# Conditioning columns as a 128-column moving operand, token loads ahead of modulation tiles, and planner costs taken from measured durations

## The chip, the cores and the metric

The kernel runs on one core of a Trainium2 chip. The metric is the device time of one execution in microseconds (us). The kernel before takes 1305.76 us, the median of three runs (1305.68 to 1306.54). Engines are called as in the profile: PE is TensorE's matmul stream, PEld its weight loads, DVE VectorE, ACT ScalarE, POOL GpSimd, SP SyncE (which issues most of the DMAs).

## The reference, cut to what matters

One layer on 512 latent tokens and 256 context tokens, width 1024, all in float32. Every sub-layer reads an RMS-normed stream that is scaled and shifted by a modulation, which is a matrix product of SiLU of a conditioning vector with one 1024 x 9216 matrix. There are two conditioning vectors: one for the tokens, one for the context.

```
mod_lat = (silu(c)     @ w_mod + b_mod)          # 9 vectors of 1024
mod_ctx = (silu(c_ctx) @ w_mod + b_mod)
adaln(h, i) = rms_norm(h) * g * (1 + mod[3i+1]) + mod[3i]
x   = x   + 0.5 * mod_lat[2] * swiglu(adaln(x, 0))      # first FFN, 2816 hidden
ctx = ctx + 0.5 * mod_ctx[2] * swiglu(adaln(ctx, 0))
y   = mixer(adaln(x, 1), adaln(ctx, 1))                 # S5 scan heads + 4 differential attention heads
x   = x + mod_lat[5] * y
x   = x + 0.5 * mod_lat[8] * swiglu(adaln(x, 2))        # second FFN, tokens only
out = rms_norm(x)
```

## The kernel before, in words

Activations lie transposed: 128 of the 1024 channels on the partitions, in eight k-tiles, 512 tokens or 256 context rows along the free axis. A product in full precision is made of three matmuls on rounded halves: weights are split into a high and a low part (`wh`, cast on ACT at L247, and `wl`, a subtraction on DVE at L252), activations too (`hh` on ACT at L139, `hl` on DVE at L142), and L294 issues high x high, low x high and high x low.

The program has four stages one after the other: the start (`begin`, from L929), the first FFN, the mixer (`enter` from L640, `attend` from L1286), and the second FFN. The windows below cut the first FFN in two, at 96 us, where the context's part of its first weights is over. On every engine instructions run in the order in which they are written. In the start and in the mixer that order is not written by hand: small operations are put into a list (`Plan`, `add`), each with an engine, a cost in us, a rank and the operations it comes after, and `Plan.run` takes, again and again, the operation that can begin first by those costs, and among equals the one with the lowest rank. So a cost or a rank is a number that changes nothing but the order. In the start, `COLD` doubles the cost of PE operations that begin before it, and `aux=2` says that two PSUM banks of that name can be in use.

The start does this:

- SP issues loads in the order of the tuple `LOADS`: `p` is a pair of modulation weight tiles (1 MB, L954 for pairs 0 to 2, L956 for 3 to 7), `a` two token k-tiles (512 KB, L959), `x` the context rows (1 MB, L992), `f` an FFN weight (512 KB, L231). The fourth FFN weight's load and those after it wait until a buffer is free, that is until the split of an earlier weight has ended on DVE; SP issues nothing behind them in the meantime.
- PE copies the conditioning columns `ct` over all partitions (L970, four times four matmuls), and ACT takes them out of PSUM (L976, tile `cb`). DVE uses `cb` for the modulation of pairs 3 to 7, by a multiply-and-sum over the free axis (L503, two per pair and conditioning vector).
- For pairs 0 to 2 PE makes the modulation itself (`products`, L1006, 16 matmuls a pair); ACT makes scale and shift of it (L995, L996).
- The tokens' squares are made on ACT (L88) and added on DVE (L95); PE sums them over the partitions (L113, eight matmuls); DVE takes the reciprocal root (L432 to L443); PE spreads it (L453) and ACT copies it out (L1075, in the tile `ssql`). Then, for k-tile after k-tile, DVE scales (L135), ACT makes `hh` (L139), DVE makes `hl` (L142), and the FFN's matmuls start (L294). The same follows for the context.

In the mixer the S5 part has eight groups of steps: PE injects (L1185), DVE scans (L1878, L1220), PE reads out (L1258 to L1260, a group is four times those three lines). The attention's key and query projections go through L1137 with weights `pwh` (ACT, L380) and `pwl` (DVE, L384), of which two can be held; `hhc`/`hlc` are the context's halves and `hhl`/`hll` the tokens'.

Of the kernel before, what the change touches and what calls it, by code (L numbers as in the profile page):

```python
# [24 lines left out]
PE_RANK = -1548  # L25
CTX_RANK = 1237
SQ_RANK = 31
WRANK = (-702, -1298, 1144, -1271, -968, -593)
# [10 lines left out]
VALUES = (-85, 757, 364)  # L39
RANKS = (43, 74, 294)  # L40
MIX = dict(PE=0.0)
S5_COSTS = (0.47,) * 6 + (0.27,) * 4 + (0.34,) * 8
# [24 lines left out]
KT = 8  # L67
# [325 lines left out]
class Layer:  # L393
# [222 lines left out]
    def enter(self, F, W, nl, nx, wp, w_st, g_st, acc_st, lat_st, ctx_st):  # L616
# [29 lines left out]
        for i, (gi, m) in enumerate(order):  # L646
# [7 lines left out]
            for ks in (range(0, 3), range(3, nj)):  # L654
                x = add(
                    "PE", len(ks) * (0.33, 0.65)[gi == 0], lambda f=product, ks=ks: f(ks), x, subs.get(m),
                    rank=-1000 + i, take=None if ks[0] else "acc",
                )
                ops.append(x)
# [92 lines left out]
        def rows(m):  # L752
# [3 lines left out]
            for v, (src, n) in enumerate(both):  # L756
# [7 lines left out]
                for k in range(KT):  # L764
                    x = add(
                        "PE", 0.65 * n / 512, lambda k=k, f=product: f(k), x, y, lows[v, k], rank=r + ROWS[2] * v + k,
                        take=None if k else "acc",
                    )
                    if k == 0:
                        take.append(x)  # L770
# [42 lines left out]
        for n in range(8):  # L813
# [40 lines left out]
            y = add("PE", 1.3, lambda n=n, t=t: t.update(o=self.s5_read(n)), x, lr[n], reads.get(n - 1), rank=r + SPACE[2], take="aux")  # L854
# [16 lines left out]
        for k in range(KT):  # L871
# [3 lines left out]
            for t in range(6):  # L875
                def product(k=k, k2=k2, kk=kk, t=t):
# [11 lines left out]
                    "PE", 0.65, product, prev.get(t), y, lows[t // 4, k], *([first[t - 1]] if k == 0 and t else ()),  # L888
# [41 lines left out]
    def begin(self, F, xl, xc, hh, hl):  # L930
        nc, a = self.nc, self.a
        sh, sc = self.mod[:, :, 0:8], self.sc[0]
        with ExitStack() as st:
# [5 lines left out]
            nc.scalar.activation(ct, ct, AF.Silu)  # L939
            nl, nx = Norm(self, xl, 512, np_, "l"), Norm(self, xc, 256, np_, "c")  # L940
# [22 lines left out]
            def spread_c(v, b):  # L963
# [10 lines left out]

                x = add("PE", 0.43, spread, rank=CB_RANK[v], take="aux")
                y = add("Activation", 0.48, lambda: nc.scalar.copy(self.cb[:, v, b * 512:(b + 1) * 512], t[0]), x)  # L976
# [21 lines left out]
            def products(j):  # L998
                t, rank = {}, 10 * j + PE_RANK

                def product(i, ks):
# [3 lines left out]
                    for k in ks:  # L1005
                        nc.tensor.matmul(  # L1006
                            t[0][:, 2 * i:2 * i + 2], w[:, k, i], ct[:, 2 * k:2 * k + 2], start=(k == 0), stop=(k == KT - 1)
                        )

                y = x = None  # L1010
                for i in range(2):
# [8 lines left out]
                    "Activation", 0.5, lambda: modulation(j, slice(0, 2), t[0][:, 0:2], t[0][:, 2:4]), x, small,  # L1020
# [8 lines left out]
            def dot(j, v):  # L1029
                rank, x = 10 * j + 4 + CTX_RANK * v, None  # L1030
                for i in range(2):
# [5 lines left out]
                    "Activation", 0.5, lambda: modulation(j, slice(v, v + 1), m[:, j:j + 1], m[:, 8 + j:9 + j]), x, small, rank=rank  # L1037
# [8 lines left out]
            for w in LOADS:  # L1046
                kind, n = w[0], int(w[1])
                if kind == "a":
                    last = add("DMA", 1.3, lambda n=n: tokens(2 * n), last, delay=2.0)
                elif kind == "x":  # L1050
                    last = add("DMA", 2.6, rows, last, delay=2.0)
                elif kind == "f":
                    if n >= F.raws:
                        weight(n - F.raws)
                    last = add("DMA", 1.3, lambda n=n: F.load(n), last, weights.get(n - F.raws), delay=2.0)
                else:
                    if n > 4:
                        dots[n - 5] = pair_dots(n - 5)
                    last = add("DMA", 2.6, lambda n=n: pair(n), last, *taken.get(n - 5, ()), delay=2.0)
# [18 lines left out]
            def stats(n, cost, loads, ranks):  # L1078
# [21 lines left out]
                return spread(n, cost, y)  # L1100

            rs = [stats(nl, 0.9, lambda k: load["a", k // 2], -1), stats(nx, 0.5, lambda k: load["x", 0], SQ_RANK)]
            done = {}
            for v, (n, o, x) in enumerate(((nl, slice(0, 512), xl), (nx, slice(512, 768), xc))):
                lows, tops = [], []
                for j in range(KT):
# [14 lines left out]
                    y = add("Activation", n.n * 0.00083 + 0.1, high, tops[-1], rank=r + 2)  # L1121
# [152 lines left out]
    def attend(self, W, unit, units, turns, banks, space, vts, T, lat_st, ctx_st):  # L1274
# [5 lines left out]
        def parts(n, src, cost, count, y, rank):  # L1280
# [7 lines left out]
            for i in range(count):  # L1288
                x = add("PE", cost, lambda i=i: go(i), y, x, banks, rank=rank, take=None if i else "mm")
                out.append(x)  # L1290
# [95 lines left out]
        def scores(g, rank):  # L1386
            h, i = divmod(g, 4)
            out = []
            for c in range(2):
# [22 lines left out]
                x = add("PE", 0.65, product, *ready[h, c], *prods[-1:], banks, rank=rank, take="s")  # L1412
# [11 lines left out]
        def probabilities(g, x0, x1, rank):  # L1424
# [17 lines left out]
            for b in range(2):  # L1442
# [18 lines left out]
                y = add("PE", 0.33, turn, x, rank=rank, take="aux")  # L1461
# [49 lines left out]
        def close(h, i, n, after, rank):  # L1511
# [6 lines left out]
            y = add("PE", 0.12 * n, lambda: rs.append(self.spread_mm(x())), y, rank=rank, take="aux")  # L1518
# [16 lines left out]
        for h, r in ((1, 40), (2, 80), (3, 120)):  # L1535
            r += RANKS[0]
# [7 lines left out]
        for g in range(16):  # L1544
            h, i = divmod(g, 4)
            rank = 100 + 10 * g
# [3 lines left out]
            else:  # L1550
                u, v = value(h, i // 2, half + got, rank + 5)
# [56 lines left out]
        def product(m, make, W, yh, yl, o, n, rank, cost, *after):  # L1608
# [7 lines left out]
            for i in range(2):  # L1616
                x = add("PE", cost / 2, lambda i=i: go(i), x, *after, rank=rank, take=None if i else "mm")
                out.append(x)
# [5 lines left out]
        for m in range(4):  # L1624
            rank = RANKS[1] + 10 + 5 * m
# [38 lines left out]
        for m in range(8 - LEFT):  # L1664
            w, l = split(m, "w2", lambda: self.W2, 4, RANKS[2] + m, after=ready)
            ops, ps = product(
                m, bank, lambda: self.W2, lambda: G["sh"], lambda: G["sl"], 0, 512, RANKS[2] + m, 2.6, l, *thirds
# [37 lines left out]
    def ffn2(self):  # L1705
# [20 lines left out]
        def out(i, m, n, cost, y, w, rank, *after):  # L1726
# [6 lines left out]
            x = add("PE", cost, product, sw, *adds[-5:-4], *after, rank=rank)  # L1733
# [82 lines left out]
        for k in range(KT):  # L1816
            for u in range(4):
                add("PE", 0.33, lambda u=u, k=k: F.mm(u, ks=[k], gis=[0]), done[0, k], weights[u], held, rank=400 + 10 * k + u)
        norm(1)
        ends = {}  # L1820
        for us in ((0, 1), (2, 3)):
            for k in range(KT):
                for u in us:
                    ends[u] = add(
                        "PE", 0.33, lambda u=u, k=k: F.mm(u, ks=[k], gis=[1]), done[1, k], weights[u], held,
# [483 lines left out]
```

## Time and profile before

| what | value |
|---|---|
| median of three runs | 1305.76 us (1305.68 to 1306.54) |
| the profiled execution's own time | 1304.25 us |
| its span | 1302.5 us |
| PE busy | 1270.3 us, 98% of the span |
| DVE busy | 838.6 us, 64% |
| ACT busy | 416.9 us, 32% |
| DMA | 169.17 MB, 130 GB/s on average |
| mean granted clock of PE | 0.978 of 2.4 GHz |

The span is the time from the first to the last instruction that the profile records; the execution's own time is 1.75 us longer. Busy shares are means over stages with different limits; so the stages stand apart in the rows below. A granted clock of 0.50 is 1.2 GHz, one of 1.00 is 2.4 GHz. "x" is a count of records; a 128-column or narrower float32 matmul of the start leaves two of them, an L294 matmul one. In a list of one engine's instructions the square brackets at the end hold the idle time before the row and what ended it.

### The profile page before, as it was taken

The numbers are of one execution on the slowest core, as the hardware profiler recorded it, in microseconds if no ns is written. First come the engines' busy times: TensorE is split into PE (matmuls) and PEld (weight loads), VectorE is DVE, ScalarE is ACT, GpSimd is POOL, SyncE is SP. The second block draws the span as 40 slices with busy tenths as digits, with TensorE's granted clock in tenths as the row PEclk, the third lists the DMA queues.
The fourth block names the chain that finished last, engine by engine and source line by source line (L and its number), as shares of the span: only waits on it lengthen the run. The fifth ranks groups of instructions, "written<-read, shape, count | busy, mean of one in ns | idle before, by whom it ended". The sixth has DMA issues, their size and how long they took to land. (4 is left out here: it accounts for less than half of the span.)

```text
span 1302.5 us, 18049 instructions
## 1 busy us (share of the span) xinstructions
PE 1270.3 (98%) x7096; PEld 1108.2 (85%) x7096; DVE 838.6 (64%) x1673; ACT 416.9 (32%) x715; POOL 55.2 (4%) x91
## 2 busy tenths in 40 slices
PE   7999999999999999999999999999999999999995
PEld 7888888888888888888888878888988888888895
DVE  4787988878777655565765988987733433333345
ACT  5341211211222221122432355864422222222223
POOL 0000001110000020110000000000000000000002
PEclk6889999999999999999999989999999999999998
DMA  9434556841453362231286543314123324223211
GB/s 351 151 121 147 200 188 250 321 138 33 128 141 91 89 198 82 104 132 40 84 303 228 186 106 70 95 49 130 59 79 105 97 62 148 82 82 120 85 55 65
DMA packets 77670, 169.17 MB, mean 130 GB/s; under 512 B 10849, under 2 KB 34401, under 8 KB 77201
## 3 DMA queue, kind: packets, MB, share of 16 engines
q1 hardware_dynamic: 66832, 130.01, 31.5%
q0 software_dynamic: 10320, 37.94, 8.1%
q8 instruction: 56, 0.92, 0.3%
q14 instruction: 30, 0.24, 0.1%
q10 hardware_dynamic: 432, 0.06, 0.0%
HBM read 146.00 MB, written 20.94 MB: 128 GB/s over the span
## 5 line engine op out<-in xcount | busy, mean ns | idle before, releaser
L294 PE MATMUL acc<-hh,wh 128*128 128x512 f32 (+1 forms) x1056 | 323.3, 353 | 0.0
L294 PE MATMUL acc<-hl,wh 128*128 128x512 f32 (+1 forms) x1056 | 321.9, 351 | 0.1
L294 PE MATMUL acc<-hh,wl 128*128 128x512 f32 (+1 forms) x1056 | 321.8, 351 | 0.0
L294 PEld LDWEIGHTS acc<-hl,wh 128*128 128x128 f32 x1056 | 178.3, 189 | 27.1 <-DVE hl L142 0.3
L294 PEld LDWEIGHTS acc<-hh,wh 128*128 128x128 f32 x1056 | 178.3, 189 | 27.0 <-issue 0.8
L294 PEld LDWEIGHTS acc<-hh,wl 128*128 128x128 f32 x1056 | 178.2, 189 | 27.0
L247 ACT CAST wh<-wraw 128x1024 fp32r<-128x1024 f32 (+3 forms) x160 | 139.8, 897 | 143.8 <-PE acc L294 106.8
L294 PE MATMUL acc<-gh,wh 128*128 128x512 f32 (+1 forms) x576 | 175.0, 342 | 0.0
L294 PE MATMUL acc<-gl,wh 128*128 128x512 f32 (+1 forms) x576 | 174.1, 340 | 0.3 <-DVE gl L314 0.3
L294 PE MATMUL acc<-gh,wl 128*128 128x512 f32 (+1 forms) x576 | 173.8, 340 | 0.0
L252 DVE TENSOR_TENSOR wl<-wraw,wh 128x1024 fp32r<-128x1024 f32 (+3 forms) x160 | 162.1, 1034 | 16.4 <-ACT wh L247 15.9
L311 DVE TENSOR_TENSOR sg<-sg,acc 128x512 f32<-128x512 f32 (+1 forms) x66 | 37.1, 588 | 189.6 <-PE acc L294 188.8
L503 DVE CUSTOM_DVE_ANT_0 junk<-wm,cb 128x1024 f32<-128x1024 f32 x100 | 122.1, 1221 | 5.2 <-DMA wm<-in_w_mod 3.9
L309 ACT ACTIVATE sg<-acc 128x512 f32<-128x512 f32 (+1 forms) x66 | 34.2, 521 | 262.0 <-PE acc L294 262.0
L294 PEld LDWEIGHTS acc<-gl,wh 128*128 128x128 f32 x576 | 98.8, 188 | 14.2 <-DVE gl L314 0.9
L294 PEld LDWEIGHTS acc<-gh,wh 128*128 128x128 f32 x576 | 98.8, 188 | 13.7 <-issue 0.8
L294 PEld LDWEIGHTS acc<-gh,wl 128*128 128x128 f32 x576 | 98.8, 188 | 13.3
L318 DVE SCALAR_TENSOR_TENSOR xl<-acc,modv,xl 128x512 f32<-128x512 f32 (+1 forms) x80 | 55.5, 694 | 63.5 <-PE acc L294 63.4
L313 ACT CAST gh<-sg 128x512 fp32r<-128x512 f32 (+2 forms) x47 | 32.6, 694 | 136.9 <-DVE sg L311 136.9
L314 DVE TENSOR_TENSOR gl<-sg,gh 128x512 fp32r<-128x512 f32 (+2 forms) x47 | 36.8, 783 | 35.7 <-ACT gh L313 35.7
L384 DVE TENSOR_TENSOR pwl<-pw,pwh 128x1024 fp32r<-128x1024 f32 (+1 forms) x26 | 25.1, 974 | 23.3 <-ACT pwh L380 23.2
L318 DVE SCALAR_TENSOR_TENSOR xc<-acc,modv,xc 128x256 f32<-128x256 f32 x40 | 19.2, 479 | 27.9 <-PE acc L294 27.8
(382 smaller groups left out, 1716.0 us busy)
## 6 DMA issues: line engine op xcount, KB each, us to landing
wraw<-in_w SPq DMA_DIRECT2D x88, 512.0 KB, 4.2
wm<-in_w_mod POOLq DMA_DIRECT2D x28, 1024.0 KB, 6.4
wraw<-in_w SPq DMA_DIRECT2D x32, 320.0 KB, 3.0
wraw<-in_w SPq DMA_DIRECT2D x24, 256.0 KB, 2.8
pw<-in_w_uqk SPq DMA_DIRECT2D x12, 512.0 KB, 3.9
wraw<-in_w SPq DMA_DIRECT2D x16, 384.0 KB, 3.2
wm<-in_w_mod SPq DMA_DIRECT2D x5, 1024.0 KB, 10.8
rot_d<-E POOLq DMA_DIRECT2D x16, 288.0 KB, 3.9
```

What stands on the lines that cost most here:

```text
L247: nc.scalar.copy(wh[:, :n], t)
L252: sub.tensor_tensor(wl[:, :n], t, wh[:, :n].bitcast(F32), op=ALU.subtract)
L294: nc.tensor.matmul(ps[gi], w, r(k)[:, o:o + n], start=(k == 0 and si == 0), stop=(k == nk - 1 and si == 2))
L309: nc.scalar.activation(sg[:, o:o + n], ps[0][gi], AF.Silu)
L311: nc.vector.tensor_mul(sg[:, o:o + n], sg[:, o:o + n], ps[1][gi])
L313: nc.scalar.copy(self.gh[j][:, o], sg[:, o])
L314: nc.vector.tensor_sub(self.gl[j][:, o], sg[:, o], self.gh[j][:, o].bitcast(F32))
L318: self.L.nc.vector.scalar_tensor_tensor(x(m), ps, gate[:, m:m + 1], x(m), op0=ALU.mult, op1=ALU.add)
L384: nc.vector.tensor_tensor(l, t, h.bitcast(F32), op=ALU.subtract)
L503: nc.vector.tensor_tensor_reduce(junk, t, self.cb[:, v], 1.0, 0.0, ALU.mult, ALU.add, self.mod[:, v, i:i + 1])
```

## The change

The moving operand of the modulation products becomes `ctw`, the same two conditioning columns repeated 64 times by a broadcast access pattern, so that each of the matmuls streams 128 columns where it streamed 2; ACT reads one copy of each. `LOADS` takes the four token pieces (and one FFN weight) ahead of the first modulation pair. The other numbers are costs, ranks and `COLD` of the planner. The changed file has three to four lines more ahead of most functions, so L1006 is L1010 there, and so on.

```diff
-LOADS = ('p0', 'a0', 'a1', 'a2', 'a3', 'f0', 'f1', 'p1', 'x0', 'f2', 'p2', 'p3', 'f3', 'f4', 'f5', 'p4', 'p5', 'p6', 'p7')
+LOADS = ('a0', 'a1', 'a2', 'f0', 'a3', 'p0', 'x0', 'p1', 'f1', 'f2', 'p2', 'p3', 'f3', 'p4', 'f4', 'p5', 'f5', 'p6', 'p7')
-COLD = 19.0
-CB_RANK = (-1461, 609)
+COLD = 12.0
+CB_RANK = (-3367, -587)
...
-S5_COSTS = (0.47,) * 6 + (0.27,) * 4 + (0.34,) * 8
+S5_COSTS = (0.49,) * 6 + (0.45,) * 4 + (0.36,) * 8
...
-            y = add("PE", 1.3, lambda n=n, t=t: t.update(o=self.s5_read(n)), x, lr[n], reads.get(n - 1), rank=r + SPACE[2], take="aux")
+            y = add("PE", 2.5, lambda n=n, t=t: t.update(o=self.s5_read(n)), x, lr[n], reads.get(n - 1), rank=r + SPACE[2], take="aux")
...
+            ctw = ct.rearrange("p (k o v) -> p k o v", k=KT, o=1).to_broadcast([128, KT, 64, 2])
...
-                            t[0][:, 2 * i:2 * i + 2], w[:, k, i], ct[:, 2 * k:2 * k + 2], start=(k == 0), stop=(k == KT - 1)
+                            t[0][:, i * 128:(i + 1) * 128], w[:, k, i], ctw[:, k], start=(k == 0), stop=(k == KT - 1)
...
-                    "Activation", 0.5, lambda: modulation(j, slice(0, 2), t[0][:, 0:2], t[0][:, 2:4]), x, small,
+                    "Activation", 0.6, lambda: modulation(j, slice(0, 2), t[0][:, 0:2], t[0][:, 128:130]), x, small,
...
-                    last = add("DMA", 1.3, lambda n=n: tokens(2 * n), last, delay=2.0)
+                    last = add("DMA", 1.3, lambda n=n: tokens(2 * n), last, delay=2.5)
...
-            rs = [stats(nl, 0.9, lambda k: load["a", k // 2], -1), stats(nx, 0.5, lambda k: load["x", 0], SQ_RANK)]
+            rs = [stats(nl, 1.5, lambda k: load["a", k // 2], -1), stats(nx, 0.8, lambda k: load["x", 0], SQ_RANK)]
```

What that does to the order is shown at three places. First SP, from the program's start; `wm` are modulation pairs, `xl` tokens, `xc` context rows, `wraw` FFN weights. Before:

```order
L954 DMA wm_116<-in_w_mod_pe 128x2048
L959 DMA xl<-in_xl 128x2x512 x4
L231 DMA wraw<-in_w 128x1024 x2
L954 DMA wm<-in_w_mod_pe 128x2048
L231 DMA wraw<-in_w 128x1024
L992 DMA xc<-in_xc 128x8x256
L231 DMA wraw<-in_w 128x1024 x2
L954 DMA wm<-in_w_mod_pe 128x2048
L956 DMA wm<-in_w_mod 128x2x1024
L231 DMA wraw<-in_w 128x1024
L956 DMA wm_328<-in_w_mod 128x2x1024
```

And now, the same engine from the same place:

```order
L963 DMA xl<-in_xl 128x2x512 x3
L234 DMA wraw<-in_w 128x1024
L963 DMA xl<-in_xl 128x2x512
L958 DMA wm_148<-in_w_mod_pe 128x2048
L996 DMA xc<-in_xc 128x8x256
L234 DMA wraw<-in_w 128x1024
L958 DMA wm<-in_w_mod_pe 128x2048
L234 DMA wraw<-in_w 128x1024 x2
L958 DMA wm<-in_w_mod_pe 128x2048
L234 DMA wraw<-in_w 128x1024
L960 DMA wm<-in_w_mod 128x2x1024
L234 DMA wraw<-in_w 128x1024
```

The tokens now stand ahead of pair 0, and the context rows ahead of pair 1. Pair 3 (the first L960, the first L956 before) now stands behind one more weight load, the fifth, which waits for a split on DVE.

Second PE, in the start, from the last two of the tokens' sums to the first FFN matmul; `rr` is the reciprocal root. Before (12 spread matmuls and the 16 of pair 0 stand ahead of the tokens' sums):

```order
L113 MATMUL aux<-ones,ssql 128x1
L113 MATMUL aux<-ones,nt 128x1
L970 MATMUL aux<-ident,ct 128x128 x4
L1006 MATMUL aux<-ct,wm 128x2 x16
L453 MATMUL aux<-ident,rr 128x128 x4
L1006 MATMUL aux<-ct,wm 128x2 x16
L113 MATMUL aux<-ones,ssqc 128x1
L113 MATMUL aux<-ones,ntc 128x1
L113 MATMUL aux<-ones,ssqc 128x1
L113 MATMUL aux<-ones,ntc 128x1
L294 MATMUL acc<-hh,wh 128x512
```

And now (all 16 spread matmuls stand ahead of the tokens' sums):

```order
L116 MATMUL aux<-ones,ssql 128x1
L116 MATMUL aux<-ones,nt 128x1
L1010 MATMUL aux<-ct,wm_148 128x128 x16
L1010 MATMUL aux<-ct,wm 128x128 x16
L456 MATMUL aux<-ident,rr 128x128 x4
L116 MATMUL aux<-ones,ssqc 128x1
L116 MATMUL aux<-ones,ntc 128x1
L116 MATMUL aux<-ones,ssqc 128x1
L116 MATMUL aux<-ones,ntc 128x1
L1010 MATMUL aux<-ct,wm 128x128 x16
L297 MATMUL acc<-hh,wh 128x512
```

Pair 0 has moved behind the tokens' sums, and the context's sums ahead of pair 2; the instructions are the same in number. The context's root is spread after 45 FFN matmuls now and after 90 before.

Third PE in the mixer, at the last S5 read and attention's key 1 (`pwh`, `pwl` with `hhl` are its first matmuls). Before:

```order
L1258 MATMUL aux<-U,toep 128x64
L1259 MATMUL aux<-F,wout 128x64
L1260 MATMUL aux<-F,wout 128x64
L1137 MATMUL mm<-hhl,pwh 128x512
L1137 MATMUL mm<-hll,pwh 128x512
L1137 MATMUL mm<-hhl,pwl 128x512
```

And now:

```order
L1141 MATMUL mm<-hhc,pwh 128x256
L1141 MATMUL mm<-hlc,pwh 128x256
L1141 MATMUL mm<-hhc,pwl 128x256
L1141 MATMUL mm<-hhl,pwh 128x512
L1141 MATMUL mm<-hll,pwh 128x512
L1141 MATMUL mm<-hhl,pwl 128x512
```

The twelve context matmuls of key 0 stood ahead of the last read and now stand between it and key 1. On DVE the rotation of key 0 (L1298 to L1303, four instructions of 128x512) has moved from between the seventh and the eighth chain of scans to behind the eighth.

## Rows read from the trace of the kernel before

**Rows 1.** The page, part 1: busy time, share of the span, instructions.
```profile
PE 1270.3 (98%) x7096; PEld 1108.2 (85%) x7096; DVE 838.6 (64%) x1673; ACT 416.9 (32%) x715; POOL 55.2 (4%) x91
```
**Rows 2.** Windows by stage: length, busy time of each engine, PE's clock, DMA share, GB/s.
```profile
0.00:38.11 38.11, 31.26 (x160) 31.21 (x161) 16.78 (x36) 18.32 (x36) 1.58 (x8) 0.65 0.81 305
38.11:96.00 57.89, 54.94 (x279) 46.45 (x280) 48.08 (x93) 22.35 (x49) 2.16 (x3) 0.90 0.41 146
96.00:600.00 504.00, 504.00 (x2952) 444.19 (x2951) 370.10 (x753) 111.20 (x166) 42.45 (x66) 1.00 0.46 147
600.00:930.00 330.00, 321.07 (x1938) 283.15 (x1937) 257.21 (x581) 160.31 (x314) 1.88 (x4) 0.98 0.40 128
930.00:1302.50 372.50, 359.04 (x1776) 303.22 (x1774) 146.44 (x212) 104.75 (x152) 7.13 (x10) 0.99 0.28 88
```
**Rows 3.** Timeline of PE in the start: start, busy us, line, count, idle before.
```profile
5.03 4.44 PE L970 MATMUL aux<-ident,ct 128*128 128x128 f32 x24 [5.03 <-ACT ct L939]
9.31 4.78 PE L1006 MATMUL aux<-ct,wm 128*128 128x2 f32 x32
15.91 0.58 PE L113 MATMUL aux<-ones,ssql 128*128 128x1 f32 x2 [1.82 <-DVE ssql L95]
...
21.19 6.83 PE L1006 MATMUL aux<-ct,wm 128*128 128x2 f32 x32
...
38.11 0.77 PE L294 MATMUL acc<-hh,wh 128*128 128x512 f32 x1
```
**Rows 4.** Windows of PE alone: length, busy (records), clock, DMA share, GB/s.
```profile
5.03:8.01 2.98, 2.98 (x14) 1.00 0.86 292
8.40:9.31 0.91, 0.91 (x10) 1.00 1.04 401
9.31:11.29 1.98, 1.98 (x21) 1.00 1.07 415
12.25:14.09 1.84, 1.84 (x9) 0.50 1.06 423
38.11:42.10 3.99, 3.99 (x11) 0.50 0.37 122
42.70:58.00 15.30, 15.30 (x67) 1.00 0.71 269
755.00:765.00 10.00, 9.28 (x34) 0.66 0.59 155
```
**Rows 5.** DMA issues, tokens (first 30 us) and POOL's (page): KB, us to landing.
```profile
xl<-in_xl SPq DMA_DIRECT2D x4, 512.0 KB, 9.1
...
wm<-in_w_mod POOLq DMA_DIRECT2D x28, 1024.0 KB, 6.4
```
**Rows 6.** Timeline of DVE in the start and the first FFN's head.
```profile
11.18 4.67 DVE L95 TENSOR_TENSOR ssql<-ssql,nt 128x512 f32<-128x512 f32 x6 [3.33 <-ACT nt L88]
...
30.58 1.42 DVE L135 SCALAR_TENSOR_TENSOR nt<-xl,sc,ssql 128x512 f32<-128x512 f32 x2 [1.92 <-ACT ssql L1075]
...
36.97 0.75 DVE L135 SCALAR_TENSOR_TENSOR nt<-xl,sc,ssql 128x512 f32<-128x512 f32 x1 [2.23 <-ACT sc L995]
...
62.81 0.75 DVE L142 SCALAR_TENSOR_TENSOR hl<-nt,modv,hh 128x512 fp32r<-128x512 f32 x1 [3.81 <-ACT hh L139]
...
84.59 0.48 DVE L142 SCALAR_TENSOR_TENSOR hl<-ntc,modv,hh 128x256 fp32r<-128x256 f32 x1 [0.64 <-ACT hh L139]
```
**Rows 7.** Window of DVE alone, first scaling to last context split.
```profile
30.58:85.07 54.49, 45.42 (x89) 0.84 0.39 143
```
**Rows 8.** Timeline of PE around the last S5 read.
```profile
753.31 0.43 PE L1259 MATMUL aux<-F,wout 128*128 128x64 f32 x2 [1.64 <-DVE F L1878]
...
758.16 0.79 PE L1137 MATMUL mm<-hhl,pwl 128*128 128x512 f32 x1 [0.72 <-DVE pwl L384]
```
**Rows 9.** Timeline of DVE there.
```profile
754.95 0.69 DVE L1301 TENSOR_TENSOR nt<-nt,ssql 128x512 f32<-128x512 f32 x1
...
756.89 2.35 DVE L384 TENSOR_TENSOR pwl<-pw,pwh 128x1024 fp32r<-128x1024 f32 x2
```

More of the change, by code (lines that the diff above doesn't have):

```diff
@@ L887, in enter @@
                 x = prev[t] = add(
-                    "PE", 0.65, product, prev.get(t), y, lows[t // 4, k], *([first[t - 1]] if k == 0 and t else ()),
+                    "PE", 0.68, product, prev.get(t), y, lows[t // 4, k], *([first[t - 1]] if k == 0 and t else ()),
                     *(outs if k == 0 else ()), rank=VALUES[0] + VALUES[1] * k + t, take=None if k else "acc",
@@ L973, in spread @@
                         )
-                x = add("PE", 0.43, spread, rank=CB_RANK[v], take="aux")
-                y = add("Activation", 0.48, lambda: nc.scalar.copy(self.cb[:, v, b * 512:(b + 1) * 512], t[0]), x)
+                x = add("PE", 0.75, spread, rank=CB_RANK[v], take="aux")
+                y = add("Activation", 0.59, lambda: nc.scalar.copy(self.cb[:, v, b * 512:(b + 1) * 512], t[0]), x)
                 x.freed = [y]
@@ L1048, in begin @@
                 if kind == "a":
-                    last = add("DMA", 1.3, lambda n=n: tokens(2 * n), last, delay=2.0)
+                    last = add("DMA", 1.3, lambda n=n: tokens(2 * n), last, delay=2.5)
                 elif kind == "x":
-                    last = add("DMA", 2.6, rows, last, delay=2.0)
+                    last = add("DMA", 2.6, rows, last, delay=2.5)
                 elif kind == "f":
@@ L1054, in begin @@
                         weight(n - F.raws)
-                    last = add("DMA", 1.3, lambda n=n: F.load(n), last, weights.get(n - F.raws), delay=2.0)
+                    last = add("DMA", 1.3, lambda n=n: F.load(n), last, weights.get(n - F.raws), delay=2.5)
                 else:
@@ L1058, in begin @@
                         dots[n - 5] = pair_dots(n - 5)
-                    last = add("DMA", 2.6, lambda n=n: pair(n), last, *taken.get(n - 5, ()), delay=2.0)
+                    last = add("DMA", 2.6, lambda n=n: pair(n), last, *taken.get(n - 5, ()), delay=2.5)
                 load[kind, n] = last
@@ L1410, in power @@
                     )
-                x = add("PE", 0.65, product, *ready[h, c], *prods[-1:], banks, rank=rank, take="s")
+                x = add("PE", 0.7, product, *ready[h, c], *prods[-1:], banks, rank=rank, take="s")
                 prods.append(x)
@@ L1616, in product @@
             for i in range(2):
-                x = add("PE", cost / 2, lambda i=i: go(i), x, *after, rank=rank, take=None if i else "mm")
+                x = add("PE", 0.525 * cost, lambda i=i: go(i), x, *after, rank=rank, take=None if i else "mm")
                 out.append(x)
@@ L1731, in product @@
                 self.out_mm(self.W2.done[w], *y(), ps[0], 256 * i, n)
-            x = add("PE", cost, product, sw, *adds[-5:-4], *after, rank=rank)
+            x = add("PE", 1.06 * cost, product, sw, *adds[-5:-4], *after, rank=rank)
             adds.append(add("DVE", n * 0.0012 + 0.07, lambda: self.out_add(m, ps[0], 256 * i, n), x, rank=rank))
```

45 lines of the change are left out of this document (24 added, 21 removed).

## The prediction

> **What bounds the kernel now.** I read the page's busy shares first: PE is busy 98% of the span and the next engine 64% [rows 1], so the time is PE's work plus what PE idles plus what it does at half clock. The windows by stage then say where those extras lie [rows 2]. Between 96 and 600 us PE is busy 504.00 of 504.00 us at clock 1.00: there nothing can be won, and whatever is won ahead of it passes through. The extras are: the start (0 to 38.11 us, clock 0.65, and none of its PE work is FFN work), the first FFN's head (57.89 − 54.94 = 2.95 us idle, clock 0.90), the mixer (330.00 − 321.07 = 8.93 us idle, clock 0.98) and the second FFN with its end (13.46 us idle). The change touches the first three; the fourth keeps its order nearly as it was.
>
> The timeline of PE in the start shows a chain [rows 3]: copies of the conditioning columns, pair 0, the tokens' sums at 15.91 us (PE waited 1.82 us for DVE's last addition), pair 1, pair 2, first FFN matmul at 38.11 us. Pairs 1 and 2 take 6.83 us each (one of the two alike rows stands there), pair 0 only 4.78. The clock explains it [rows 4]: 21 records in 1.98 us in pair 0's first half (0.094 us a record), 9 in 1.84 us shortly after (0.204), where the row shows 0.50. PE had streamed 2-column matmuls without a gap when its clock fell, at about 11.7 us. From there it stays at 1.2 GHz, through both other pairs, until 42.10 us, four us into the FFN's 512-column matmuls (11 records in 3.99 us there, 67 in 15.30 after).
>
> **The change part by part.**
>
> *Wide moving operand.* 128 columns against 2 cost the same at each level: the 128-column copies of `ct` run at 0.213 us a record at first (14 in 2.98 us, the pace of 1.2 GHz, though no clock change has been recorded yet and the row reads 1.00) and at 0.091 later (10 in 0.91 us); the 2-column ones at 0.204 and 0.094 [rows 4]. Widening adds 0. What it may give is clock. Two wide streams raised it, 128 columns after some 3.2 us (from 5.03 to about 8.2, between the first two rows) and 512 columns after 3.99 us [rows 4]. I take 4 us for the pairs, the longer of the two.
>
> The Trainium skill ("TensorE: Matmul & The Clock Gate", Part 1) says that the clock follows how busy PE has been recently, and names no width. By that the wide operand would change nothing, since PE had no gap in pair 0. The trace of before speaks against it: the clock fell in a gapless stream of 2 columns.
>
> *Tokens first.* Tokens need 9.1 us from issue to landing, beside pair 0's 1 MB [rows 5]. At 415 GB/s [rows 4] that megabyte is 2.5 us; of these one FFN weight (0.5 MB, 1.2 us) now stands ahead of the last token piece. So the first tokens land 2.5 us sooner and the last about 1.7. DVE adds from 11.18 on, six additions in 4.67 us [rows 6], which ends at 15.85; 2.5 sooner is 13.3. I take 12.7, because ACT's first square also no longer stands behind three copies of `cb`. The sums are 8 × 0.43 = 3.4 us, from 12.7 to 16.1.
>
> *PE after that.* Pair 0 runs 16.1 to 21.5: four us at 0.427 a matmul (9.4 matmuls), the other 6.6 at 0.21. Pair 1 is 16 × 0.21 = 3.4 us, to 24.9, if it has landed; it now follows 5 MB (four token pieces, a weight, pair 0, context, a weight) instead of 3.5, and 1.5 MB at 415 GB/s is 3.6 us, so it lands at about 21.4 against 18. Root spread 0.9 us, to 25.8; ACT's copy of it to about 27.3, since two weight casts and pair 1's scale stand ahead of it; context sums 1.7 us at half, about 0.9 at full clock; pair 2, 3.4 us. With a little loss between them the first FFN matmul comes at 30 to 31 us, against 38.11. It also begins at 1.00: the 3.99 us at half clock [rows 4] hold 9.35 matmuls, which gain 0.19 us each, 1.8 us. PE alone would be some 9 us early.
>
> *What is late next.* That is DVE. It scales, splits and makes the modulation of pairs 3 to 7 between 30.58 and 85.07 us, busy 45.42 of 54.49 us [rows 7], and at the end of that stretch PE waits for it (part of the 2.95 us). Of its 9.07 us idle, 3.81 wait for an ACT operation at 62.81 [rows 6] that stands in ACT's queue behind the context root's copy, which waits for PE's spread; that spread now comes 45 matmuls sooner, so I cost this wait at nothing. So I do with the 0.64 at 84.59, and with the 2.23 at 36.97 for pair 2's scale, which PE now makes before DVE asks [rows 6]. Left are 2.4 us in small waits. New is pair 3: it is queued on SP behind the fifth weight's load, which waits for the second split on DVE at about 26, so it is issued at about 26.7. Its landing takes between 2.5 us (1 MB at 415 GB/s, nothing beside it) and 9.1 (the tokens, with a megabyte beside them); I take 6.3, near the 6.4 of the 28 like tiles that POOL issues later [rows 5]: 33. DVE, which could start its first product for pair 3 at 31, idles 2.0 us. Its first scaling is at about 27.4, behind ACT's copy (30.58 before), so the last context split ends at 27.4 + 45.4 + 2.0 + 2.4 = 77.2, against 85.07: 7.9, say 8.0 us early. PE gets there sooner and waits, and the whole first FFN shifts by 8.0. By the bounds: pair 3 landing 9.1 us after its issue leaves some 5; DVE without any wait gives 12.4, but PE cannot give more than its 9 to 10. So −4 to −10, with −8.0 taken.
>
> *Mixer.* Here no instruction is added or taken away. The last read waited 1.64 us for DVE's `F`, key 1 then 0.72 us for the split `pwl` [rows 8], and the two together dropped the clock: 9.28 us of work in 10.00 at 0.66 [rows 4], that is 3.4 us at most, of which 0.7 is the wait itself. Now the twelve context matmuls of key 0 stand between the last read and key 1, and the key's rotation leaves DVE's way, so `F` comes some 2.7 us (four operations of the form that takes 0.69 [rows 9]) sooner, at 750.6: the 1.64 goes. But the casts and splits for key 1 need the weight buffers that those twelve matmuls hold. The read then ends at about 753.0 and the twelve at 754.5 (0.12 us each); a split takes 1.2 us (half of 2.35 [rows 9]) and a cast, taken to be as long, too, so the first `pwl` is there at 756.9 and not at 758.0. So one wait of about 2 us takes the place of the two, with half clock behind it as before: gain about 1. The other reorderings (injections earlier, key weight splits in pairs) have no row of their own: between −4 (half of the 8.93 us idle goes) and +4 (as much again comes); I take −0.5, near nothing. Mixer −1.5.
>
> *Second FFN.* Costs 5% higher on all its PE operations leave the order alone but for neighbours: 0, with ±1.
>
> *Sum.* 1304.25 − 8.0 − 1.5 = 1294.75 for an execution like the profiled one. That one lies 1.51 us under the median of the runs; on the median's scale 1305.76 − 9.5 = 1296.3 us.
>
> **Rivals.**
> 1. *The mixer's stall goes altogether.* For it: the wait's causes are both moved; against it: two weight buffers tie key 1's split to the end of key 0. If key 1's weights are ready, 1.64 + 0.72 and about 3.0 us at half clock are saved: 5.4 in place of 1.0, so 1296.3 − 4.4 = 1291.9.
> 2. *The queue takes the start's gain.* For it: three weights wait for splits ahead of pairs 3 to 5 on SP, and nothing passes them; DVE's own products then wait as the pairs do. Against it: 48.08 of 57.89 us busy [rows 2] leaves DVE room to catch up. A further 4 us of waits on pairs 4 to 7 leave 4 of 8.0: 1300.3.
> 3. *The clock follows busy time, not width.* Mechanism here: pair 0 starts at 1.2 GHz behind a gap and narrow sums and stays there. Pairs cost 6.83 each [rows 3]: 16.1 to 22.9, 29.7, root to 31.6, context sums 33.3, pair 2 to 40.1, so the FFN starts 2 us later than before. But DVE starts its scaling at about 32.5 and loses no 3.81, and its last split ends at about 82 against 85.07: −3 from the start, −1 from the mixer, 1301.8. For it: no row shows a 128-column stream of DMA-fed weights at 2.4 GHz that began at 1.2. Against it: the two wide streams above.
> 4. *Slower: exposed key splits.* With the splits of a key's weights paired on DVE and tied to the previous key's matmuls, PE stands before key 2 and key 3 as before key 1. One such place costs 2.4 us idle and 3.0 at half clock, 5.4; two more are +10.8, and the mixer's −1.5 is not had: 1305.76 − 8.0 + 10.8 = 1308.6. It decides from 8.0 us more idle and half clock in the mixer on. For it: the mixer's DVE is busy 257.21 of 330.00 us [rows 2]; against it: only key 1 shows such a wait before.
> 5. That the change doesn't do what it says would be the wide products costing more than the narrow ones; the paces in [rows 4] exclude that beyond 0.02 us a matmul, 1 us in all.
>
> **How the numbers follow.** My forecast has 50%, its own range is 1292.5 to 1300 (start −5 to −10, mixer +1 to −4). Rival 1 has 17%, rival 2 14%, rival 3 11%, rival 4 8%. No change means within 0.2% (1303.15 to 1308.37), about what a measurement of this kernel can tell. Faster: all of the forecast but 1 in 50, all of rival 1, 11 of rival 2's 14, 7 of rival 3's 11, none of rival 4: 0.49 + 0.17 + 0.11 + 0.07 = 0.84, of which I give 2 to the rest for reorderings that no row prices: 0.82. Rival 4 is split, 4 and 4; with the remainders same is 0.11 and slower 0.07. The range, from rival 1's centre less 2 to rival 3's plus 1.7, is 1290 to 1303.5: below it lie some 6 in 100 and above some 14.
>
> **What would show it right or wrong.** In the profile after: the first L297 matmul at 30 to 31 us and its first records at clock 1.00; pair 0's later half and pairs 1 and 2 at 0.1 us a record (at 0.2, rival 3 holds); the tokens' sums at about 12.7; DVE's last context split at about 77, with a wait for pair 3 near 31 (waits for pairs 4 to 7: rival 2); from there to the mixer a constant shift of 8. In the mixer no wait for `F` at the last read, and one of about 2 us before key 1 (none: rival 1; two more: rival 4). The forecast is wrong if PE's first FFN matmul comes after 35, or if the mixer is longer by more than 4 us.

## The result, and the profile after

The changed kernel takes 1313.46 us, the median of six runs (1310.84 to 1315.93), against 1306.15 before (six runs, 1305.35 to 1308.65). The ratio is 1.0053, 95% interval 1.0038 to 1.0068: slower by half a per cent, 17 us away from the 1296.3 that was forecast, and outside the range. The two profiled executions took 1304.25 us before and 1310.84 after, the lowest of its six; they lie 6.6 us apart where the medians lie 7.3 apart.

The trace divides that into a gain and a larger loss. The windows of the changed kernel by stage, with columns as in [rows 2], cut at its first FFN matmul (29.80 us in place of 38.11):

```profile
0.00:29.80 29.80, 20.79 (x161) 20.22 (x161) 15.23 (x36) 16.54 (x32) 1.57 (x8) 1.00 0.93 333
29.80:96.00 66.20, 62.58 (x342) 53.42 (x341) 57.43 (x105) 28.05 (x58) 2.15 (x3) 0.97 0.48 169
96.00:600.00 504.00, 504.00 (x2933) 443.37 (x2932) 366.38 (x747) 108.88 (x162) 42.33 (x66) 1.00 0.46 145
601.93:940.86 338.93, 319.80 (x1917) 280.52 (x1916) 258.00 (x583) 160.38 (x316) 2.15 (x4) 0.97 0.40 125
```

and the mixer of the kernel before between the same two operations:

```profile
611.84:933.86 322.02, 313.09 (x1914) 277.04 (x1913) 255.93 (x583) 160.14 (x316) 1.88 (x4) 0.98 0.41 131
```

The stretch begins at ACT's last square ahead of the first FFN's end (611.84 before, 601.93 after) and ends at ACT's last `hh` at the head of the second FFN (933.86 and 940.86). So the first FFN ends 9.91 us sooner, and the mixer takes 338.93 us in place of 322.02, 16.91 more. PE idles 19.13 of them in place of 8.93, 10.2 more. Its granted clock is at 1.2 GHz for 20.5 us of the stretch in place of 10.2, which by the doubled time of a matmul costs about 5.1 more. Some 1.6 us are left. From there to the end the two traces run alike: ACT's last square comes at 1287.86 before and at 1294.48 after, 353.62 to 354.00 us behind the last `hh`.

**The start** went as forecast, and better. PE's timeline after, against [rows 3]:

```profile
12.77 0.38 PE L116 MATMUL aux<-ones,ssql 128*128 128x1 f32 x2 [0.89 <-DVE ssql L98]
...
14.57 3.82 PE L1010 MATMUL aux<-ct,wm 128*128 128x128 f32 x32
20.00 3.81 PE L1010 MATMUL aux<-ct,wm 128*128 128x128 f32 x32 [1.61 <-DMA wm<-in_w_mod_pe]
...
26.23 3.81 PE L1010 MATMUL aux<-ct,wm 128*128 128x128 f32 x32 [0.74 <-DMA wm<-in_w_mod_pe]
29.80 0.48 PE L297 MATMUL acc<-hh,wh 128*128 128x512 f32 x1
```

The tokens' sums start at 12.77 us (12.7 forecast). All three pairs take 3.8 us where two took 6.83, with two short waits for their data, and the first FFN matmul runs at full clock. That the tokens' sums and pair 0 ran at 2.4 GHz too is chance: in all six other profiled executions with this start (e1, e4 to e6, e8 and, but for one load, e9 below) the clock fell between 10.0 and 14.9 us, and rose again between 18.3 and 22.2 us, within the wide pairs. DVE's timeline, against [rows 6]:

```profile
25.36 0.75 DVE L138 SCALAR_TENSOR_TENSOR nt<-xl,sc,ssql 128x512 f32<-128x512 f32 x1 [0.61 <-ACT ssql L1079]
...
31.79 1.22 DVE L506 CUSTOM_DVE_ANT_0 junk<-wm,cb 128x1024 f32<-128x1024 f32 x1 [3.28 <-DMA wm<-in_w_mod]
...
73.93 0.48 DVE L145 SCALAR_TENSOR_TENSOR hl<-ntc,modv,hh 128x256 fp32r<-128x256 f32 x1 [0.64 <-ACT hh L142]
```

The wait for pair 3 is there (3.28 us, 2.0 forecast), the waits of 3.81 and 2.23 us are gone, and the last context split starts at 73.93 where it started at 84.59: 10.7 us sooner. The window of DVE from the first scaling to that split's end, against [rows 7]:

```profile
25.36:74.42 49.06, 44.98 (x90) 1.00 0.55 200
```

**The mixer** is where the time went. PE's timeline after, its longer waits from the scan to the last head:

```profile
724.29 0.43 PE L1262 MATMUL aux<-U,toep 128*128 128x64 f32 x2 [0.73 <-ACT S L1196]
...
753.45 0.50 PE L1141 MATMUL mm<-hhl,pwh 128*128 128x512 f32 x1 [1.41 <-ACT pwh L383]
754.71 0.50 PE L1141 MATMUL mm<-hhl,pwl 128*128 128x512 f32 x1 [0.53 <-DVE pwl L387]
...
825.29 0.80 PE L1401 MATMUL s<-kh,qs 128*128 128x512 f32 x1 [3.21 <-ACT e L1412]
...
828.21 1.54 PE L1453 MATMUL aux<-ident,e 128*128 128x128 f32 x6 [1.27 <-DVE e L1437]
...
888.14 0.84 PE L1453 MATMUL aux<-ident,e 128*128 128x128 f32 x6 [1.69 <-DVE rv L439]
```

At key 1 the waits are as forecast: none at the last read, 1.41 + 0.53 = 1.94 us before the key (about 2 forecast). The half clock that was forecast behind them did not come. It stands earlier, behind waits of 0.73 and 0.37 us in the scan. Windows of PE after, first there and then at key 1 ([rows 4] has 0.66 for that place before):

```profile
725.00:735.00 10.00, 9.63 (x45) 0.66 0.69 247
753.00:763.00 10.00, 8.88 (x48) 1.00 0.71 162
```

From the end of the first FFN to key 1's first `pwl`, PE has the same 874 matmuls in both kernels. Its window before and then after:

```profile
611.84:758.16 146.32, 139.91 (x874) 0.98 0.53 183
```

```profile
601.93:754.71 152.78, 144.17 (x874) 0.96 0.52 176
```

So 6.46 us were lost by then, though the place itself shows no longer wait: 2.2 us more idle in small waits, and most of the rest at half clock. Some 2 us of it come back behind key 1, where the kernel before still ran at 1.2 GHz.

The large new place is at 822 to 830 us, in the last attention head. The window there, PE alone, in the kernel after:

```profile
820.00:830.00 10.00, 5.04 (x19) 0.75 1.07 287
```

PE works half of those ten microseconds, and part of that at 1.2 GHz. What it lacks there is the S5 part's gated unit, 48 matmuls that fill this place in the kernel before. Its operands `g` are loaded by SP as soon as the last key's context product has ended (the planner's `open_g` comes after all four keys): in before, after, e1, e2, e4 and e6 alike the load is issued 0.3 us after the last matmul of that product has started. SP's timeline before and then after; the third number is the time that the issues take:

```profile
808.88 2.88 SPq L1699 DMA_DIRECT2D g<-g_d  x4
```

```profile
818.38 3.48 SPq L1703 DMA_DIRECT2D g<-g_d  x4
```

and ACT's copy of that last product (`kr`) and its cast of `g` after:

```profile
818.38 0.37 ACT L1341 COPY kr<-mm 128x256 f32<-128x256 f32 x1 [2.55 <-PE mm L1141]
...
825.14 2.16 ACT L1605 CAST ggh<-g 128x512 fp32r<-128x512 f32 x4
```

The load starts in the same hundredth of a microsecond in which the product's copy starts. The work around it comes sooner than before (the first exponential at 768.30 against 773.84, the score products ahead of it by 4 to 7 us); this load comes 9.5 us later. PE's timeline has the gated unit's first matmul at 821.80 before and at 831.93 after:

```profile
821.80 0.39 PE L1683 MATMUL mm<-ggh,pwh 128*128 128x512 f32 x1
```

```profile
831.93 0.58 PE L1687 MATMUL mm<-ggh,pwh 128*128 128x512 f32 x1
```

In the order of the instructions the reason reads: before, the last key's context product stood behind 12 of the 32 score products (each counted by its `kh` matmul on 512 keys), now it stands behind 14; the gated unit stood behind 16 and now stands behind 18.

### The profile page after: what moved, and what is told of

Its sections match the earlier page's. It is cut to its first block, busy times and chain, and to the rows that moved or that the text cites. A ratio compares the mean times of both kernels' runs of the same rounds, so it can differ in the third digit from the quotient of the medians.

```text
span 1309.1 us, 18050 instructions
## 1 busy us (share of the span) xinstructions
PE 1263.9 (97%) x7096; PEld 1098.3 (84%) x7096; DVE 840.3 (64%) x1673; ACT 416.8 (32%) x715; POOL 55.3 (4%) x91
```

## Experiments

The nine runs below were timed against the kernel before on the same chip, whose median was 1306.07, 1305.35 and 1307.08 us in the three sets (e1 to e4, e5 to e7, e8 and e9). All have the whole computation. This table, from ACT's timelines of the profiled executions, cuts each mixer at the first exponential: leg 1 is from the last square of the first FFN to there, leg 2 from there to the last `hh`. "Key 3" is the number of score products ahead of the last key's context product. The legs are those of one execution each. Most of these lie within 1.1 us of their run's median; after (2.6) and e4 (2.4) lie below it, as does before (1.9), and e3 (3.1) and e5 (3.8) above.

```
kernel              median   ratio (95%)              1st FFN ends  leg 1   leg 2   key 3
before              1306.15                           611.84        162.00  160.02  12
after               1313.46  1.0053 (1.0038-1.0068)   601.93        166.37  172.56  14
e1 start only       1296.18  0.9922 (0.9907-0.9937)   602.18        163.27  160.06  12
e2 mixer only       1322.60  1.0128 (1.0109-1.0148)   613.60        166.12  173.06  14
e3 narrow           1319.50  1.0099 (1.0082-1.0116)   609.19        169.94  173.23  14
e4 key 3 earlier    1308.73  1.0025 (1.0016-1.0035)   603.60        163.79  168.95  10
e5 scan costs       1301.08  0.9974 (0.9961-0.9987)   603.43        167.36  163.64  12
e6 score cost       1304.82  0.9996 (0.9986-1.0005)   601.31        163.15  170.60  14
e7 wide only        1299.84  0.9957 (0.9943-0.9971)   606.39        163.73  160.07  12
e8 attention costs  1308.01  1.0012 (1.0001-1.0023)   602.65        163.17  173.11  14
e9 pair 3 first     1294.84  0.9900 (0.9880-0.9920)   600.82        162.00  161.99  12
```

**e1, the start alone.** Wide operand, `LOADS`, `COLD`, the start's ranks and costs as changed; these and all like them put back:

```diff
-S5_COSTS = (0.49,) * 6 + (0.45,) * 4 + (0.36,) * 8
+S5_COSTS = (0.47,) * 6 + (0.27,) * 4 + (0.34,) * 8
...
-                x = add("PE", 0.7, product, *ready[h, c], *prods[-1:], banks, rank=rank, take="s")
+                x = add("PE", 0.65, product, *ready[h, c], *prods[-1:], banks, rank=rank, take="s")
```

Expected: 

> Wide operand, load order and the start's ranks and costs as changed; the mixer's and the second FFN's costs as before, so their order on PE is that of before. Theory A (the changed planner costs make a worse mixer order, and the start keeps what it won): the 9.9 us that the first FFN ends earlier stay to the end, 1306.15 - 9.9 = about 1296. Rival B (an earlier start is given back in the mixer whatever its order, because loads and the clock's level meet it at another time): 1306 to 1313, with new waits in the mixer.

Measured: 1296.18 us. The start's 9.9 us stay to the end; leg 2 is that of before to within 0.04 us. Leg 1 is 1.3 us longer here with the same instructions in the same order, as the clock stayed at 1.2 GHz for 13.7 us of it in place of 10.2. The loads of `g` (SP's timeline) and the gated unit's first matmul (813.46) have moved with everything else:

```profile
800.54 3.06 SPq L1703 DMA_DIRECT2D g<-g_d  x4
```

Theory A holds, rival B (an earlier start is given back whatever the order) falls.

**e2, the mixer alone.** The other half of the change: all costs and ranks from `enter` on as changed, the start as before.

```diff
-                x = add("PE", 0.65, product, *ready[h, c], *prods[-1:], banks, rank=rank, take="s")
+                x = add("PE", 0.7, product, *ready[h, c], *prods[-1:], banks, rank=rank, take="s")
...
-                y = add("PE", 0.33, turn, x, rank=rank, take="aux")
+                y = add("PE", 0.55, turn, x, rank=rank, take="aux")
```

Expected: 

> The start as before, the mixer's and the second FFN's costs as changed. Theory A: the traces lose 16.5 us between the mixer's begin and the end, so 1306.15 + 16.5 = about 1322.5, with PE waiting 3 us or more for ACT's exponential ahead of the gated unit's product. Rival B: no loss without the earlier start, 1306 within 3.

Measured: 1322.60 us, 16.5 more than before, with both legs as long as in the changed kernel within 0.5 us and the same 3.21 us wait for the exponential (at 836.94). The two halves of the change are independent: −9.9 and +16.5 make +6.6, and the two together measure +7.3.

**e3, the narrow operand in the changed kernel.**

```diff
-                            t[0][:, i * 128:(i + 1) * 128], w[:, k, i], ctw[:, k], start=(k == 0), stop=(k == KT - 1)
+                            t[0][:, 2 * i:2 * i + 2], w[:, k, i], ct[:, 2 * k:2 * k + 2], start=(k == 0), stop=(k == KT - 1)
```

Expected: 

> The changed kernel with the 2-column moving operand put back; load order, costs and ranks as changed. Theory A1 (the clock stays up because of the 128 columns): pairs 1 and 2 fall back to 0.2 us a record, 6.8 us each in place of 3.8, and the first FFN matmul comes at 36 to 38 us in place of 29.8; DVE hides some, so the first FFN ends 4 to 8 us later than in the changed kernel and the time is 1317 to 1321. Rival A2 (the new order alone keeps the clock up or the time down): 1313.5 within 2.

Measured: 1319.50 us, 6.0 more than with the wide operand. Windows of PE: pairs 0 and 1, pair 2, the first FFN matmuls; columns as in [rows 4]:

```profile
14.17:27.82 13.65, 13.65 (x65) 0.50 0.92 344
31.24:38.06 6.82, 6.82 (x33) 0.50 0.81 331
38.06:41.20 3.14, 3.14 (x9) 0.50 0.01 3
```

PE has no gap in 13.65 us and stays at 1.2 GHz; the FFN starts at 38.06. In e1 the clock had fallen too, in the gaps at about 10 us, and pairs 0 and 1 show what 128 columns do then (copies and sums, pair 0's first 4.09 us, the rest of the two pairs):

```profile
10.44:16.21 5.77, 5.51 (x25) 0.50 1.04 388
16.21:20.30 4.09, 4.09 (x20) 0.51 1.02 416
20.30:25.37 5.07, 5.07 (x48) 1.00 0.86 347
```

20 records in 4.09 us, then 48 in 5.07. Theory A1 holds: in the same order of instructions the 2-column pairs stayed at 1.2 GHz to their end, and the 128-column ones came back to 2.4. The rule of the Trainium skill ("TensorE: Matmul & The Clock Gate", Part 1) that the clock follows how busy PE is, read with the busy share of this profile, does not tell these two streams apart: both are 1.00. The measurement decides.

**e4, key 3 earlier.** One number of the changed kernel.

```diff
-HEADS = (85, 125, 165)
+HEADS = (85, 125, 140)
```

Expected: 

> The changed kernel with one number changed: rank 140 in place of 165 for the last attention head, so that its key's context product stands after 10 score products and not after 14 (12 for its last half before the change). Theory A3 (the loads of the gated unit's operands wait for the last key's weight buffers, so a late key 3 leaves PE without work at 822 to 829 us): that stall and its half clock go, 6 to 9 us: 1305 to 1307. Rival A4 (the loss is spread over many small reorderings and the stall only gathers it): 1312 to 1314, the waits reappear elsewhere.

Measured: 1308.73 us, 4.7 less than the changed kernel. That is between the two expectations. The loads of `g` are issued at 808.79 and the gated unit starts at 820.93; the 3.21 us are gone, but other waits stand in the head (PE's timeline):

```profile
811.53 0.50 PE L1401 MATMUL s<-kh,qs 128*128 128x512 f32 x1 [1.38 <-ACT e L1412]
813.88 0.65 PE L1401 MATMUL s<-kh,qs 128*128 128x512 f32 x1 [1.39 <-ACT e L1412]
```

Leg 2 gains 3.6 us of the 12.5 that it had lost. Leg 1 is 2.6 us shorter as well, but not by this number: up to 790 us PE, DVE and ACT run the same instructions in the same order as in the changed kernel, and this execution spent 3.4 us of leg 1 at 1.2 GHz where that one spent 13.7. Its first FFN, with the same order too, ended 1.7 us later. So key 3's place accounts for the one large stall and not for all of leg 2; both theories were half right.

**e5, the scan's costs alone** (with the new start): `S5_COSTS`, the read's 2.5, the input products' costs.

```diff
-            y = add("PE", 1.3, lambda n=n, t=t: t.update(o=self.s5_read(n)), x, lr[n], reads.get(n - 1), rank=r + SPACE[2], take="aux")
+            y = add("PE", 2.5, lambda n=n, t=t: t.update(o=self.s5_read(n)), x, lr[n], reads.get(n - 1), rank=r + SPACE[2], take="aux")
```

Expected: 

> The start as changed; of the planner's other costs only those of the mixer's input products and of the S5 scan as changed; attention, gated unit and second FFN as before (key 3's last product after 12 score products, as before the change). Theory C1 (two separate losses: some 3 us ahead of the first exponential by the scan's order, 12 us by attention's): 1296.2 + 3 = 1299 to 1300.5. Rival C2 (the scan's costs carry the whole loss, since they set when attention begins): 1308 or more.

Measured: 1301.08 us, 4.9 more than e1, 0.6 above C1's range and with a wide spread of single runs (1298.89 to 1307.13). Rival C2 falls. The profiled execution took 1304.85 us, so its trace shows more loss than the median has. Its leg 1 is 1 us longer than in the changed kernel and ends in a wait of 2.91 us for the `kh` transfer ahead of the first scores (PE's timeline), which may be no part of a usual execution:

```profile
768.26 0.47 PE L1401 MATMUL s<-kh,qs 128*128 128x512 f32 x1 [2.91 <-DMA kh<-kh]
```

Leg 2 is 3.6 us longer than in e1, but PE idles no longer there: it has 18 more matmuls in it (17 of them 512-column projections at 0.23 us, 3.9 us together), which stand ahead of the first exponential in e1. PE's window of leg 2 in e1 and then in e5:

```profile
765.45:925.51 160.06, 157.07 (x970) 1.00 0.29 82
```

```profile
770.79:934.43 163.64, 161.61 (x988) 0.99 0.28 81
```

So the scan's costs lose their time in leg 1.

**e6, one cost.** The new start and a score product at 0.70 in place of 0.65.

```diff
-                x = add("PE", 0.65, product, *ready[h, c], *prods[-1:], banks, rank=rank, take="s")
+                x = add("PE", 0.7, product, *ready[h, c], *prods[-1:], banks, rank=rank, take="s")
```

Expected: 

> The start as changed and one cost of the mixer: a score product at 0.70 in place of 0.65. That alone puts key 3's products behind 14 score products (12 before) and the gated unit's behind 19 (16 before). Theory A3 (key 3's place is what costs): most of attention's 12 us comes back, 1303 to 1308, with PE waiting for an exponential or the gated unit's operands. Rival D (one cost that is off by 0.05 us is nothing; it takes many): 1296 within 2.

Measured: 1304.82 us, 8.6 more than e1 (9.4 when each is taken against the kernel before of its own set), all of it in leg 2 (170.60 against 160.06 in the traces). The loads of `g` are issued at 811.31, 10.8 us later than in e1, and PE waits (its timeline):

```profile
815.69 1.13 PE L456 MATMUL aux<-ident,sums 128*128 128x128 f32 x8 [2.58 <-DVE sums L446]
820.70 0.50 PE L1401 MATMUL s<-kh,qs 128*128 128x512 f32 x1 [2.83 <-ACT e L1412]
```

Rival D falls: 0.05 us in one cost takes back nearly the whole gain of the start.

**e7, the wide operand alone** in the kernel before.

```diff
-                            t[0][:, 2 * i:2 * i + 2], w[:, k, i], ct[:, 2 * k:2 * k + 2], start=(k == 0), stop=(k == KT - 1)
+                            t[0][:, i * 128:(i + 1) * 128], w[:, k, i], ctw[:, k], start=(k == 0), stop=(k == KT - 1)
```

Expected: 

> The kernel before with the 128-column operand alone; load order, costs and ranks as before. Theory E1 (the widening gives its clock alone, and DVE's first scaling, some 3 us earlier, sets what is left): pairs 1 and 2 take 3.8 us each, the first FFN matmul comes at 31 to 33 us, the time is 1301 to 1303. Rival E2 (in the old order narrow sums behind pair 0 drop the clock again): 1306 within 1.5. Rival E3 (all of the start's gain is the operand's): 1296 to 1298.

Measured: 1299.84 us, 1.2 us better than E1 allowed and 1.8 worse than E3; E2 falls. PE's timeline has pairs 1 and 2 and the first FFN matmul here:

```profile
23.40 4.49 PE L1007 MATMUL aux<-ct,wm 128*128 128x128 f32 x32
...
28.75 3.81 PE L1007 MATMUL aux<-ct,wm 128*128 128x128 f32 x32
...
33.20 0.47 PE L294 MATMUL acc<-hh,wh 128*128 128x512 f32 x1
```

By the end of the first FFN the operand alone gives 5.45 us, the new order alone (e3) 2.65, both 9.91.

**e8, attention's costs** (and those of the gated unit and the second FFN) with the new start; the complement of e5.

```diff
-                y = add("PE", 0.33, turn, x, rank=rank, take="aux")
+                y = add("PE", 0.55, turn, x, rank=rank, take="aux")
...
-                x = add("PE", 0.65, product, *ready[h, c], *prods[-1:], banks, rank=rank, take="s")
+                x = add("PE", 0.7, product, *ready[h, c], *prods[-1:], banks, rank=rank, take="s")
```

Expected: 

> The start as changed; the costs and ranks of attention, of the gated unit and of the second FFN as changed, those of the input products and the scan as before. Theory C1 (two losses that add): the whole loss beside the start is 17.3 us (1313.5 - 1296.2) and the scan's share 4.9 (1301.1 - 1296.2), so 1296.2 + 12.4 = 1308.6, with key 3 behind 14 score products and the gated unit's loads at some 10 us later than in the start's run. Rival C3 (the losses do not add, since each order only meets the other's): 1303 or less, or 1312 or more.

Measured: 1308.01 us (1308.6 expected by C1). Leg 1 is that of e1, leg 2 that of the changed kernel, with the same wait (PE's timeline):

```profile
821.70 0.50 PE L1401 MATMUL s<-kh,qs 128*128 128x512 f32 x1 [3.21 <-ACT e L1412]
...
828.45 0.99 PE L1687 MATMUL mm<-ggh,pwh 128*128 128x512 f32 x1
```

The two losses add: 4.9 (e5) + 11.8 (e8) = 16.7 of the 17.3 us that the changed kernel lies above e1; each taken against the kernel before of its own set, 5.6 + 10.8 = 16.4 of 17.2.

**e9, pair 3 ahead of the third weight**, on e1.

```diff
-LOADS = ('a0', 'a1', 'a2', 'f0', 'a3', 'p0', 'x0', 'p1', 'f1', 'f2', 'p2', 'p3', 'f3', 'p4', 'f4', 'p5', 'f5', 'p6', 'p7')
+LOADS = ('a0', 'a1', 'a2', 'f0', 'a3', 'p0', 'x0', 'p1', 'f1', 'p2', 'p3', 'f2', 'f3', 'p4', 'f4', 'p5', 'f5', 'p6', 'p7')
```

Expected: 

> As the run of the start alone (1296.2 us), with the load of modulation pair 3 right behind pair 2 and ahead of the third FFN weight, so that it no longer stands behind a load that waits for a split. Theory F1 (DVE sets the end of the first FFN's head, and its wait for pair 3, 1.5 us in the run of the start alone and 3.3 in the changed kernel, goes): 1293 to 1295. Rival F2 (the FFN weights come late instead and PE waits for their splits): 1297 or more. Rival F3 (DVE meets another wait at once): 1296 within 1.

Measured: 1294.84 us. The time is F1's, but its interval overlaps that of e1, and the trace speaks for F3: DVE's wait for pair 3 is gone, other waits stand in its place, and the last context split starts at 74.16 us, not sooner than in e1 (73.92). DVE's timeline:

```profile
26.12 1.41 DVE L138 SCALAR_TENSOR_TENSOR nt<-xl,sc,ssql 128x512 f32<-128x512 f32 x2 [1.47 <-ACT ssql L1079]
31.25 0.75 DVE L138 SCALAR_TENSOR_TENSOR nt<-xl,sc,ssql 128x512 f32<-128x512 f32 x1 [1.17 <-ACT sc L999]
...
74.16 0.48 DVE L145 SCALAR_TENSOR_TENSOR hl<-ntc,modv,hh 128x256 fp32r<-128x256 f32 x1 [0.64 <-ACT hh L142]
```

Whether e9 is better than e1 stays open. Both are faster than the kernel before and the changed one: the start of the change with the mixer's order of before is the version to take.

## Why the prediction was wrong

**The start was right in its mechanism, and near in its size.** The term was −8.0 and measured −9.9 at the first FFN's end, −9.9 in the time of e1. The wide pairs ran at 2.4 GHz, or came back to it, and with the 2-column operand of e3 they did not; PE was ahead and DVE set the end of the head, as forecast. The 1.9 us that were missing came out of DVE's chain: its last context split ended at 74.4 us, 2.8 sooner than the 77.2 of the forecast. Its first product for pair 3 came at 31.8 where 33 was forecast, and its small waits came to 0.8 us (49.06 − 44.98 − 3.28) where 2.4 was taken. That its first scaling came at 25.36 where 27.4 was forecast gave nothing. In e1, where pair 0 began at 1.2 GHz, it came at 27.08; DVE then waited 1.54 us for pair 3 in place of 3.28, and its last split started at 73.92 all the same. DVE's timeline of e1:

```profile
27.08 0.75 DVE L138 SCALAR_TENSOR_TENSOR nt<-xl,sc,ssql 128x512 f32<-128x512 f32 x1 [0.34 <-ACT ssql L1079]
...
31.77 1.23 DVE L506 CUSTOM_DVE_ANT_0 junk<-wm,cb 128x1024 f32<-128x1024 f32 x1 [1.54 <-DMA wm<-in_w_mod]
```

One input of the sum was misread: before, pair 1 followed 4 MB and not 3.5; after, PE had it at 20.0 us where 21.4 was forecast. That the time of the whole forecast, 1296.3, is that of e1 is luck: it counts 1.5 us from the mixer, which e1 leaves as it was.

**The step that failed is the mixer's term.** The prediction priced one place there, the last read and key 1, and the waits of that place were as it said (one of 1.94 us for two). For "the other reorderings" it wrote that they "have no row of their own: between −4 (half of the 8.93 us idle goes) and +4 (as much again comes); I take −0.5, near nothing". The mixer came to +16.9 us in the trace and +16.5 in e2, four times the bound; one more than 4 us longer was the prediction's own sign of being wrong. The bound was worked out from the waits of an order that was about to be replaced: the 8.93 us of idle time say how well the old order fits, and nothing of how badly a new one can.

What it passed over could be read before the run. The order shows the last key's context product moved from behind 12 score products to behind 14, and the planner's `open_g` shows who waits for it; what this costs could have been bounded, as an estimate, by what stood in that place, 48 matmuls of the gated unit at 0.23 us, 11 us. The forecast followed two places of the order through and took the rest as noise around zero.

**Rival 4 had the sign and the kind, not the place.** It held that an exposed wait in the attention costs its idle time plus half a clock behind it, 5.4 us a place, and decides from 8 us on. The mechanism was right: in the changed kernel the wait of 3.21 us in the last head was followed by 6.8 us at half clock (825.0 to 831.8), in which the wait of 1.27 us lies. The mixer's 10.2 us more of idle time and 5.1 more at half clock are well past its 8. But it put the waits at the key splits of heads 2 and 3, where none appeared, and gave the case 8 in 100. Rivals 2 and 3 fell with e1 and e3. Rival 1 fell with the wait at key 1, though the half clock that it counted on saving there is gone.

**What stays open.** Leg 2 lost 12.5 us. PE's window there before and then after:

```profile
773.84:933.86 160.02, 157.64 (x973) 1.00 0.29 82
```

```profile
768.30:940.86 172.56, 163.33 (x983) 0.98 0.26 76
```

Idle time rose by 6.9 us (from 2.38 to 9.23), and half clock took about 3.4. Most of the other 2.3 is work that changed sides: ten more matmuls stand in this leg, seven of them 512-column projections that stood in leg 1 before. Which of the smaller reorderings make up the 9 us that e4 still lies above the old leg 2 was not tried, nor which of the scan's costs loses its time ahead of key 1.

## What to carry to other kernels

A planner's costs are knobs for an order and not estimates to be set right: ranks that were tuned under one set of costs fit that set, and a set taken from measured durations made a worse order; one cost changed by 0.05 us was worth 8.6 us. When such numbers change, compare the orders first and follow each load that opens late (who waits for its buffer, what it was to fill), before pricing any of it at zero. And time the parts of a combined change by themselves: here the start alone was worth −9.9 us and the rest +16.5.

## What the runs showed of the hardware

Two gapless streams of the same products ran at different granted clocks: 13.65 us of 2-column matmuls stayed at 1.2 GHz from beginning to end (e3), while in e1 the clock rose to 2.4 GHz 4 us into the 128-column pairs. In e7 it rose at 25.0 us, when PE had run 128-column copies and pair 1 without a gap from 21.55 on. The wide matmul cost nothing more. Pair 0 at 2.4 GHz, PE's timeline of e2 (2 columns; its clock fell at 13.7 us, at the last record) and of e7 (128 columns):

```profile
10.36 3.75 PE L1009 MATMUL aux<-ct,wm 128*128 128x2 f32 x32
```

```profile
11.52 3.74 PE L1007 MATMUL aux<-ct,wm 128*128 128x128 f32 x32
```

At 1.2 GHz it is 20 records in 4.09 us (e1), 0.204 each, the pace of the narrow ones in [rows 4].
